# Seven quarter products in the second feed-forward of a two-layer decoder trunk

## The chip, the cores and the metric

The kernel runs on one core of one Trainium2 chip. The metric is the device time of one execution in microseconds, the median over several runs. TensorE (PE) multiplies matrices out of on-chip memory (SBUF) into accumulation banks (PSUM), VectorE (DVE) and ScalarE (ACT) work on elements, GpSimd (POOL) and SyncE (SP) issue transfers between main memory and SBUF here. Each engine takes its instructions in one fixed order and waits on semaphores for what the others produce.

## The reference

A sequence of 512 tokens of width 1024 goes through two layers. Each layer is a token mixer and then a feed-forward, each followed by a residual sum and a layer norm:

```python
x = layer_norm(DEEPNORM_ALPHA * x + mix, ln1_g[layer], ln1_b[layer])
ffn = sqrelu_mlp(x, ffn_w1[layer], ffn_b1[layer], ffn_w2[layer], ffn_b2[layer])
x = layer_norm(DEEPNORM_ALPHA * x + ffn, ln2_g[layer], ln2_b[layer])

def sqrelu_mlp(x, w1, b1, w2, b2):
    return jnp.square(jax.nn.relu(x @ w1 + b1)) @ w2 + b2
```

`w1` is 1024 x 4096 and `w2` 4096 x 1024, all in float32. The first layer's mixer is a state-space group beside stick-breaking attention, the second's a convolution module. The change concerns the second layer's feed-forward alone, above all its last product, squared hidden (512 x 4096) times `w2`.

## The kernel before

Every float32 product runs as three matmuls of a reduced 32-bit type. An operand is split into a high part (a cast on ScalarE, line 101 for weights, 215 for activations) and a low part, the rest (a subtraction on VectorE, lines 102 and 216); the product is high x high + low x high + high x low. One matmul takes a stationary 128 x 128 operand and streams 512 columns past it.

The inner dimension of 4096 is cut into 32 tiles of 128. In the second layer they go in blocks of 8, 8, 6, 4 and 6 (line 40). For each tile of a block `ffn1` (line 1033) computes the hidden tile, features by tokens, with 8 x 3 = 24 matmuls (`gemm`, line 219; named f in the profile), then Relu (ScalarE), square (VectorE) and the split. After that the block's part of the output product follows (line 1311, named g): tokens are the stationary operand, four token blocks of 128, and 512 output columns of `w2` stream by, once for each half of the columns. Each of the eight results (4 token blocks x 2 halves) is added by VectorE (line 1314) to one of eight tiles XT of 128 tokens x 512 columns, which hold the scaled residual. The last block (line 1327, named h) goes token block by token block, with the layer norm and the writing of its rows behind each.

Ahead of the first block stands the *lead*: while the layer norm of the second half of the tokens is computed, TensorE already does the first six hidden tiles (LEAD = 6; named fl), first for the one half of the tokens, then for the other. Then `residual` (line 1276) scales x and turns it into tokens by features with 32 transposes on TensorE (line 1284, named xt), copied to XT by ScalarE (line 1287).

Weights come through the class `Weights`: a list of units in the order of use, each 128 x 1024 elements. `next` hands out a unit and prepares those up to five ahead (`ahead`): load by SP (line 71, two buffers of 1 MB named raw), cast, subtraction, into a ring of eight slots. The order of the instructions on each engine is made by a scheduler when the program is built.

Of the kernel before, what the change touches and what calls it, by code (L numbers as in the profile page):

```python
# [39 lines left out]
FFN_BLOCKS = ((8, 8, 8, 8), (8, 8, 6, 4, 6))  # L40
# [15 lines left out]
class Weights:  # L56


    def __init__(self, tc, ahead):
        self.tc, self.nc, self.ahead = tc, tc.nc, ahead  # L60
        self.slots, self.units, self.raw, self.urgent, self.fence, self.hold = [], [], None, True, None, False
        self.done, self.got, self.chunk, self.ready, self.kept = 0, 0, {}, {}, {}

# [3 lines left out]
    def fetch(self, i):  # L67
        key, src, nk, ncol, off, width = self.units[i]
        if key not in self.chunk:
            self.chunk[key] = self.raw.tile([P, nk, width], F32, tag="raw", name=f"raw{i}", bufs=2)  # L70
            self.nc.sync.dma_start(self.chunk[key], src)
# [8 lines left out]
    def _prep(self, n):  # L80
        nc = self.nc
        while self.done < min(n, len(self.units)):
            key, src, nk, ncol, off, width = self.units[self.done]
            if key[0] == "split":
                pool, s = self.slots[self.done % len(self.slots)]
# [6 lines left out]
            self.fetch(self.done)  # L92
            raw = self.chunk[key][:, :, off : off + ncol]
            pool, s = self.slots[self.done % len(self.slots)]
# [12 lines left out]
            self.done += 1  # L107

# [57 lines left out]
def kernel(ctx: ExitStack, tc: tile.TileContext, a: dict, out: bass.AP):  # L166
# [63 lines left out]
    wpool = ctx.enter_context(tc.tile_pool(name="mw", bufs=1))  # L230
# [600 lines left out]
    wp2 = ctx.enter_context(tc.tile_pool(name="w2", bufs=1))  # L831
    hid = ctx.enter_context(tc.tile_pool(name="hid", bufs=1))
# [30 lines left out]
    for layer in range(2):  # L863
        if layer:
            units += [(("split", i), None, 8, 128, 0, 0) for i in range(24 + LEAD)]
        k0 = 0
        for nb in FFN_BLOCKS[layer]:
            for m in range(k0, k0 + nb, 4):
                units += units_of(f"f1{layer}", a["ffn_w1"][layer], 0, 8, range(max(m, LEAD * layer) * P, min(m + 4, k0 + nb) * P, 128), 256)
                if layer == 0 and m >= KEEP_FROM:  # L870
# [3 lines left out]
            for j in range(0, KT, 4) if layer == 0 else ():  # L874
# [6 lines left out]
            if layer == 0:  # L881
                pass
            else:
                for c in (0, 512):
                    for k in range(k0, k0 + nb, 2):
                        units += units_of("f21", a["ffn_w2"][1], k, 2, [c], 512)
# [383 lines left out]
    W.ahead = AHEAD[0]  # L1270
    xs, first = tail_norm_lead(cs_, "d", None, ("ln1_g", 8), ("ln1_b", 8), LEAD, "fl1", the_rest)


    XT = [None] * KT

# [13 lines left out]
    def ffn2_tok(ps, hs, b, ws, f):  # L1289
# [91 lines left out]
```

## Time and profile before

| | |
|---|---|
| median of 3 runs | 1185.39 us (1182.16 to 1188.67) |
| profiled execution, first to last instruction | 1181.7 us; the page gives no other time for it |
| TensorE matmuls | busy 1154.5 us, 98% |
| VectorE | busy 752.0 us, 64% |
| ScalarE | busy 507.9 us, 43% |
| mean granted TensorE clock | 0.995 |
| second layer's feed-forward | from the lead's last part at 839.92 us to the end |

Busy matmuls are pipelined, so a busy TensorE is not one at its peak; the spacing of its matmuls is read from the chain of waits. An operation's mean duration is longer than the step from one to the next in a queue. Shares over the whole span mix stages, so the stretches from 840 us on are the ones to look at.

### The profile page before, as it was taken

To read this page: it belongs to the slowest core of one execution; us is meant where nothing else is said; L and a number is where in the kernel's file an instruction comes from. 1 tells how busy PE (TensorE), PEld (TensorE's weight loads), DVE (VectorE), ACT (ScalarE), POOL (GpSimd) and SP (SyncE) were. 2 spreads that over 40 slices of the span, in tenths; PEclk is the share of its full clock that TensorE was granted. 3 is DMA by queue.
4 is the path that set the end of the run, shared out by engine and by line. 5 is a ranking of instruction groups with operands and counts; after the bars stand their busy time and mean duration, and the time that the engine had idled before them with its cause. 6 is when DMAs were issued, how large, how long until landed. Compare 5 with 4: busy or idle time off the path is not lost.

```text
span 1181.7 us, 17927 instructions
## 1 busy us (share of the span) xinstructions
PE 1154.5 (98%) x7252; PEld 966.1 (82%) x7252; DVE 752.0 (64%) x1332; ACT 507.9 (43%) x802; POOL 66.5 (6%) x125
## 2 busy tenths in 40 slices
PE   9989999999999999999999999899999999999997
PEld 7777767799888888888999776699988888888885
DVE  7999875498546546546565999886933433434446
ACT  6857769345434435434323122662741422413220
POOL 1022210000000000000021110001000000000000
PEclk9999999999999999999999999999999999999999
DMA  8511221332689678788464641215242232323211
GB/s 211 166 55 50 81 81 46 109 114 72 223 292 299 228 281 298 249 292 290 134 213 153 205 164 58 68 44 172 90 143 72 89 125 72 109 91 104 78 47 72
DMA packets 132547, 169.60 MB, mean 144 GB/s; under 512 B 13874, under 2 KB 105778, under 8 KB 132464
## 3 DMA queue, kind: packets, MB, share of 16 engines
q1 hardware_dynamic: 123664, 136.96, 36.0%
q0 software_dynamic: 8640, 31.46, 7.9%
q8 instruction: 57, 0.93, 0.3%
q14 instruction: 26, 0.21, 0.1%
q10 hardware_dynamic: 160, 0.03, 0.0%
HBM read 132.12 MB, written 35.65 MB: 142 GB/s over the span
## 4 chain that ended last, share of the span: by engine, by line
PE 83%; ACT 2%; DVE 1%; DMA 1%; issue 1%; POOL 0%; SPq 0%; DVEq 0%; ACTq 0%
PE f L225 24%; PE g L1311 12%; PE acf L225 11%; PE fl L225 5%; PE tlb L225 4%; PE tld L225 4%; PE pv L225 3%; PE h L1295 3%; PE pg L225 3%; PE cw L1126 3%; PE tla L225 2%; PE pl L225 2%; PE acmo L225 1%; PE gg L225 1%; PE gv L225 1%
## 5 line engine op out<-in xcount | busy, mean ns | idle before, releaser
L102 DVE TENSOR_TENSOR wlo<-raw,whi 128x1024 fp32r<-128x1024 f32 x176 | 213.3, 1223 | 196.1 <-ACT whi L101 193.0
L101 ACT CAST whi<-raw 128x1024 fp32r<-128x1024 f32 x176 | 182.3, 1050 | 319.6 <-PE g L1311 107.0
L1311 PE MATMUL g<-whi,hh 128*128 128x512 f32 x208 | 81.7, 393 | 0.0
L1311 PE MATMUL g<-whi,hl 128*128 128x512 f32 x208 | 81.6, 392 | 0.0
L1311 PE MATMUL g<-wlo,hh 128*128 128x512 f32 x208 | 81.6, 392 | 0.0
L225 PE MATMUL f<-xah,whi 128*128 128x512 f32 x208 | 81.0, 390 | 0.0
L225 PE MATMUL f<-xdh,whi 128*128 128x512 f32 x208 | 81.0, 389 | 0.0
L225 PE MATMUL f<-xdl,whi 128*128 128x512 f32 x208 | 80.9, 389 | 0.0
L225 PE MATMUL f<-xal,whi 128*128 128x512 f32 x208 | 80.9, 389 | 0.0
L225 PE MATMUL f<-xdh,wlo 128*128 128x512 f32 x208 | 80.9, 389 | 0.0
L225 PE MATMUL f<-xah,wlo 128*128 128x512 f32 x208 | 80.9, 389 | 0.0
L225 PE MATMUL acf<-hh,whi 128*128 128x512 f32 x192 | 75.6, 394 | 0.0
L225 PE MATMUL acf<-hl,whi 128*128 128x512 f32 x192 | 75.5, 393 | 0.0
L225 PE MATMUL acf<-hh,wlo 128*128 128x512 f32 x192 | 75.4, 393 | 0.0
L215 ACT CAST hh<-fr 128x512 fp32r<-128x512 f32 x64 | 39.7, 621 | 59.1 <-DVE fr L353 59.1
L216 DVE TENSOR_TENSOR hl<-fr,hh 128x512 fp32r<-128x512 f32 x64 | 44.1, 690 | 31.1 <-ACT hh L215 31.1
L353 DVE TENSOR_TENSOR fr<-fr 128x512 f32<-128x512 f32 x64 | 43.6, 684 | 16.7 <-ACT fr L154 16.7
L357 DVE SCALAR_TENSOR_TENSOR cy<-hp,wdw,cy 128x512 f32<-128x512 f32 (+1 forms) x75 | 49.3, 657 | 0.8 <-ACT cy L154 0.8
L88 POOL DMA_DIRECT2D whi<-kepth x30 | 16.0, 535 | 549.5 <-PE tlb L225 385.9
L1311 PEld LDWEIGHTS g<-whi,hh 128*128 128x128 f32 x208 | 39.1, 188 | 8.8
L1311 PEld LDWEIGHTS g<-wlo,hh 128*128 128x128 f32 x208 | 39.1, 188 | 8.8
L1311 PEld LDWEIGHTS g<-whi,hl 128*128 128x128 f32 x208 | 39.0, 188 | 8.8
(631 smaller groups left out, 2891.9 us busy)
## 6 DMA issues: line engine op xcount, KB each, us to landing
raw<-in_ffn_w_dram SPq DMA_DIRECT2D x48, 1024.0 KB, 5.5
raw<-in_ffn_w_dram SPq DMA_DIRECT2D x32, 512.0 KB, 3.8
kepth<-whi SPq DMA_DIRECT2D x30, 512.0 KB, 3.2
keptl<-wlo SPq DMA_DIRECT2D x30, 512.0 KB, 9.2
whi<-kepth POOLq DMA_DIRECT2D x30, 512.0 KB, 3.6
wlo<-keptl POOLq DMA_DIRECT2D x30, 512.0 KB, 4.6
raw<-in_conv_w_pw_dram SPq DMA_DIRECT2D x12, 1024.0 KB, 6.5
raw<-in_mix_w_in_dram SPq DMA_DIRECT2D x16, 512.0 KB, 4.2
```

The costliest lines, as they stand in the source:

```text
L88: nc.gpsimd.dma_start(x, d)
L101: i0 = nc.scalar.copy(hi, raw).ins
L102: i1 = nc.vector.tensor_sub(lo, raw, hi.bitcast(F32)).ins
L215: i0 = S.copy(hi, src).ins
L216: i1 = V.tensor_sub(lo, src, hi.bitcast(F32)).ins
L225: ins = PE.matmul(ps[:, c0:c1], u[:, k, ksl], v[:, c0:c1], start=start and k == 0 and i == 0, stop=stop and k == n - 1 and i == 2).ins
L353: V.tensor_tensor(o, x, y, op=op)
L357: V.scalar_tensor_tensor(o, x, s, y, op0=op0, op1=op1)
L1126: PE.matmul(cps[j, c0][g][C, :], Ds[j][t // 16][R, t % 16, :], hps[j][R, t + c0 : t + c1], start=t < 4, stop=t >= n - 4, tile_position=(R. ...
L1295: PE.matmul(ps, u, v, start=k == 0 and i == 0, stop=k == nk - 1 and i == 2)
L1311: PE.matmul(pss[b], u, v[:, kk, :], start=k + kk == 0 and i == 0, stop=k + kk == nb - 1 and i == 2)
```

## The change

For the first 24 of the 32 inner tiles the output product is formed after Strassen's identity. The blocks are now 6, 6, 6, 6 and 8. In a block of six the tiles are taken as three pairs (e = 0, 1). A pair's hidden tile is split by token half, the weights by the pair's tile and by column half, so that a 2 x 2 times 2 x 2 block product arises, formed from seven quarter products in place of eight. A quarter product of a block is 2 token blocks x 3 pairs x 3 = 18 matmuls.

- On the hidden side (`pair`) a tile q of 8 slots of 256 tokens holds the four quarters and four sums or differences; seven of them are split into high and low, three in one cast and one subtraction (768 elements), four in another (1024). The square moved from VectorE to ScalarE.
- On the weight side four quarters of 128 x 3 x 512 elements are loaded per block by SP (`load_quads`); `operand` forms four differences in place on VectorE, and each of the seven operands is split (1536 elements). The ring has four slots, `ahead` is 3.
- `seven` goes through the products in the order 1, 2, 5, 6, 3, 7, 4. Product 3 goes on adding into the bank of product 5, products 7 and 4 into that of product 6, and VectorE adds a bank to XT after each step, 12 sums per block. Product 1 is collected in R1 and added to all eight XT tiles in the last block of six.
- The pools of the weights are closed and three new ones opened at the turn to the second layer's feed-forward. Hidden weights there are loaded in single units of 512 KB.
- Block 0 has only the lead's six hidden tiles. The last block, of eight tiles, does the first column half for all token blocks, then the second by token block.

```diff
-FFN_BLOCKS = ((8, 8, 8, 8), (8, 8, 6, 4, 6))
+FFN_BLOCKS = ((8, 8, 8, 8), (6, 6, 6, 6, 8))
+ORDER7 = (1, 2, 5, 6, 3, 7, 4)
+NB = 6
+NSLOT = 4
...
+            if key[0] == "quad":
+                raw = self.operand(*key[1:])
+            else:
+                self.fetch(self.done)
+                raw = self.chunk[key][:, :, off : off + ncol]
...
+    def load_quads(self, blk, w2, k0, nb):
+        src = w2[k0 * P : (k0 + nb) * P].rearrange("(k e p) (f n) -> e f p k n", e=2, p=P, f=2)
+        q = self.quads[blk] = {}
+        for e, f in ((0, 0), (1, 0), (0, 1), (1, 1)):
+            q[e, f] = self.raw.tile([P, nb // 2, T], F32, tag=f"quad{e}{f}", name=f"quad{blk}{e}{f}", bufs=1)
+            self.nc.sync.dma_start(q[e, f], src[e, f])
+    def operand(self, blk, i):
+        q, sub = self.quads[blk], self.nc.vector.tensor_sub
+        b11, b12, b21, b22 = q[0, 0], q[0, 1], q[1, 0], q[1, 1]
+        if i == 5:
+            sub(b11, b12, b11)
+        elif i == 6:
+            sub(b11, b22, b11)
+        elif i == 7:
+            sub(b12, b22, b12)
+        elif i == 4:
+            sub(b21, b21, b11)
+        return {1: b11, 2: b21, 5: b11, 6: b11, 3: b22, 7: b12, 4: b21}[i]
...
+    def turn():
+        wst.close()
+        pools = [ctx.enter_context(tc.tile_pool(name=f"w3{x}", bufs=1, reuse_waits="tile")) for x in "abc"]
+        W.slots, W.base, W.raw, W.ahead = [], W.done, pools[1], NSLOT - 1
...
+    def pair(m, pss):
+        q = f1.tile([P, 8, H], F32, tag="q", name=f"q{m}", bufs=2)
+        hi, lo = (f1.tile([P, 7, H], F32R, tag=f"a{x}", name=f"a{x}{m}", bufs=NB // 2) for x in "hl")
+        for e in range(2):
+            r = rect(m + e, pss[e] if pss else hidden(m + e)).rearrange("p (h c) -> p h c", h=2)
+            act(q[:, 1:3] if e else q[:, 0:8:7], r, AF.Square)
+        split_part(hi[:, 0:3], lo[:, 0:3], q[:, 0:3])
+        tt(q[:, 3], q[:, 7], q[:, 2], ALU.add)
+        tt(q[:, 4], q[:, 3], q[:, 0], ALU.subtract)
+        tt(q[:, 5], q[:, 0], q[:, 7], ALU.subtract)
+        tt(q[:, 6], q[:, 1], q[:, 4], ALU.subtract)
+        split_part(hi[:, 3:7], lo[:, 3:7], q[:, 3:7])
+        return hi, lo
...
+    def seven(blk, As, first, final):
+        for i in ORDER7:
+            wh, wl = W.next()
+            chain = {3: 5, 7: 6, 4: 6}.get(i, i)
+            for t in range(2):
...
+                for p, (ah, al) in enumerate(As):
+                    uh, ul = ah[:, PLACE[i], c], al[:, PLACE[i], c]
+                    for n_, (u, v) in enumerate(((uh, wh), (ul, wh), (uh, wl))):
+                        PE.matmul(ps, u, v[:, p, :], start=chain == i and p == 0 and n_ == 0, stop=p == len(As) - 1 and n_ == 2,
+                                  skip_group_check=True)
...
+                    for x in (2 * t, 2 * t + 1, 2 * t + 4, 2 * t + 5) if final else ():
+                        tt(XT[x], XT[x], R1[t], ALU.add)
+                else:
+                    x = 2 * t + {2: 0, 5: 5, 6: 1, 3: 1, 7: 5, 4: 4}[i]
+                    tt(XT[x], XT[x], ps, ALU.add)
...
     k0 = 0
-    for bi, nb in enumerate(FFN_BLOCKS[1]):
-        hs = ffn1(1, bi, k0, nb, xs, stp, first if bi == 0 else ())
+    for bi, nb in enumerate(FFN_BLOCKS[1][:-1]):
+        if bi:
+            W.load_quads(k0, a["ffn_w2"][1], k0, nb)
+        As = [pair(m, first[m : m + 2] if bi == 0 else None) for m in range(k0, k0 + nb, 2)]
         if bi == 0:
             residual()
+        seven(k0, As, bi == 0, bi == len(FFN_BLOCKS[1]) - 2)
```

Up to the end of the lead every engine's order is the same in both kernels, but for two weight units that ScalarE and VectorE prepared there before and no longer do. Three places of the new order follow; line numbers are those of the changed kernel.

ScalarE, after the lead's last hidden tile (fl15, turned to r15). Names: q4 and ah4 are the third pair's tile and its high parts, xt the transposed X, whi152 and whi153 the high parts of the first two quarter weights. In the changed kernel:

```order
L185 ACTIVATE r15_8689<-fl15_8447,PV_86 128x512
L185 ACTIVATE q4_8683<-r15_8689 128x512
L1356 CAST ah4_8684<-q4_8683 128x768
L1337 COPY X0_61<-xt00_8716 128x512
L1337 COPY X1_62<-xt10_8717 128x512
L1337 COPY X2_63<-xt20_8718 128x512
L1356 CAST ah4_8684<-q4_8683 128x1024
L110 CAST whi152_8635<-quad000_8627 128x1536
L1337 COPY X3_64<-xt30_8719 128x512
L1337 COPY X4_65<-xt01_8740 128x512
L110 CAST whi153_8639<-quad010_8629 128x1536
```

Before, the same stretch was this, with TensorE at hidden tiles 6 and 7 (f16, f17) meanwhile:

```order
L154 ACTIVATE fr15_8661<-fl15_8447,PV_86 128x512
L101 CAST whi158_8727<-raw158_8725 128x1024
L215 CAST hh15_8664<-fr15_8661 128x512
L101 CAST whi159_8832<-raw159_8830 128x1024
L154 ACTIVATE fr16_8717<-f16_8668,PV_86 128x512
```

The copies of X have moved up, and the first weights of the product stand behind them.

VectorE in the first block of products (wlo152 to wlo156: low parts of the weights of products 1, 2, 5, 6 and 3; quad: the differences; X: sums into the output):

```order
L111 TENSOR_TENSOR wlo152_8636<-quad000_8627,whi152_8635 128x1536
L111 TENSOR_TENSOR wlo153_8640<-quad010_8629,whi153_8639 128x1536
L131 TENSOR_TENSOR quad000_8627<-quad001_8631,quad000_8627 128x1536
L135 TENSOR_TENSOR quad001_8631<-quad011_8633,quad001_8631 128x1536
L111 TENSOR_TENSOR wlo156_8797<-quad011_8633,whi156_8796 128x1536
L111 TENSOR_TENSOR wlo154_8766<-quad000_8627,whi154_8765 128x1536
L385 TENSOR_TENSOR X0_61<-X0_61,s020_8800 128x512
L133 TENSOR_TENSOR quad000_8627<-quad011_8633,quad000_8627 128x1536
L385 TENSOR_TENSOR X1_62<-X1_62,s021_8810 128x512
L111 TENSOR_TENSOR wlo157_8824<-quad001_8631,whi157_8823 128x1536
L111 TENSOR_TENSOR wlo155_8771<-quad000_8627,whi155_8770 128x1536
```

Of this only the sums into X were there before. The low parts for product 3 (wlo156) and product 7 (wlo157) stand ahead of those that products 5 and 6 need first.

TensorE in the last block of products (s186: bank of product 6, s185: of products 5 and 3, f124: hidden tile 24):

```order
L1390 MATMUL s1861_10147<-whi194_10045,al22_9970 128x512
L1390 MATMUL s1861_10147<-wlo194_10046,ah22_9969 128x512
L256 MATMUL f124_10239<-xdh0_7955,whi198_10161 128x512
L256 MATMUL f124_10239<-xdl0_7956,whi198_10161 128x512
L1390 MATMUL s1850_10110<-whi195_10079,ah18_9813 128x512
L1390 MATMUL s1850_10110<-whi195_10079,al18_9814 128x512
```

Two of the 24 matmuls of tile 24 stand between products 6 and 3; the other 22 follow after product 4. Before, hidden tiles and output products did not mix.

More of the change, by code (lines that the diff above doesn't have):

```diff
@@ L873 @@
                     n += 2
-            for j in range(0, KT, 4) if layer == 0 else ():
+            for j in range(0, KT, 4):
                 units += units_of("f20", a["ffn_w2"][0], k0, nb, range(j * P, (j + 4) * P, 128), 256)
@@ L880 @@
                     n += m
[L881 to L886, printed above, removed]
             k0 += nb
@@ L1287, in residual @@
                 S.copy(X[4 * f + b], pss[b])
-    def ffn2_tok(ps, hs, b, ws, f):
-        nk = len(hs)
-        for k in range(nk):
-            hh, hl = (t_[:, b * P : (b + 1) * P] for t_ in hs[k])
-            wh, wl = (t_[:, k % 2, :] for t_ in ws[k // 2])
-            for i, (u, v) in enumerate(((hh, wh), (hl, wh), (hh, wl))):
-                PE.matmul(ps, u, v, start=k == 0 and i == 0, stop=k == nk - 1 and i == 2)
+    hst.close()
+    f1 = ctx.enter_context(tc.tile_pool(name="f1", bufs=1, side="right", reuse_waits="tile"))
@@ new lines, with rect, hidden, split_part @@
+    R1 = [page(f"R1{t}", F32) for t in range(2)]
+    def rect(m, ps):
+        r = page(f"r1{m}", F32)
+        act(r, ps, AF.Relu, bias=pv("ffn_b1", 32 + m))
+        return r
+    def hidden(m):
+        ps = stp(f"f1{m}")
+        gemm(ps, W.next(), slice(0, P), xs, 0, T)
+        return ps
+    def split_part(hi, lo, src):
+        S.copy(hi, src)
+        V.tensor_sub(lo, src, hi.bitcast(F32))
+    def pair(m, pss):
[11 more added lines that the diff above has]
+        return hi, lo
@@ new lines @@
+    PLACE = {1: 0, 2: 1, 4: 2, 5: 3, 6: 4, 7: 5, 3: 6}
+    def seven(blk, As, first, final):
+        bank = {}
+        for i in ORDER7:
+            wh, wl = W.next()
+            chain = {3: 5, 7: 6, 4: 6}.get(i, i)
+            for t in range(2):
+                if chain == i:
+                    bank[i, t] = nps(f"s{blk}{i}{t}")
+                ps = bank[chain, t]
+                c = slice(t * P, (t + 1) * P)
+                for p, (ah, al) in enumerate(As):
[3 more added lines that the diff above has]
+                                  skip_group_check=True)
+            for t in range(2):
+                ps = bank[chain, t]
+                if i == 1:
+                    if first:
+                        S.copy(R1[t], ps)
+                    else:
+                        tt(R1[t], R1[t], ps, ALU.add)
+                    for x in (2 * t, 2 * t + 1, 2 * t + 4, 2 * t + 5) if final else ():
+                        tt(XT[x], XT[x], R1[t], ALU.add)
+                else:
+                    x = 2 * t + {2: 0, 5: 5, 6: 1, 3: 1, 7: 5, 4: 4}[i]
+                    tt(XT[x], XT[x], ps, ALU.add)
@@ L1316 @@
+    hs = []
+    for i in range(nb_last):
+        if i % 3 == 0:
+            hl_ = [f1.tile([P, 3, T], F32R, tag=f"a{x}", name=f"b{x}{i}", bufs=NB // 2) for x in "hl"]
+        r = rect(k0 + i, hidden(k0 + i))
+        act(r, r, AF.Square)
+        hs.append(tuple(x[:, i % 3, :] for x in hl_))
+        split_part(*hs[-1], r)
     gb = []
```

85 lines of the change are left out of this document (53 added, 32 removed).

## The prediction

> **What bounds the kernel now.** I read the page's busy times first, then busy time by stretch, then the chain of waits.
>
> ```profile
> span 1181.7 us, 17927 instructions
> ...
> PE 1154.5 (98%) x7252; PEld 966.1 (82%) x7252; DVE 752.0 (64%) x1332; ACT 507.9 (43%) x802; POOL 66.5 (6%) x125
> ```
>
> ```profile
> 850.00:900.00 50.00, 49.98 (x241) 41.47 (x240) 20.06 (x24) 18.71 (x26) 0.00 (x0) 1.00 0.40 127
> 900.00:950.00 50.00, 50.00 (x221) 41.20 (x220) 22.18 (x26) 17.29 (x22) 0.00 (x0) 1.00 0.27 84
> 1050.00:1100.00 50.00, 50.00 (x220) 40.94 (x219) 21.52 (x25) 14.28 (x17) 0.00 (x0) 1.00 0.31 96
> ```
>
> In these stretches of the second feed-forward (busy PE, PEld, DVE, ACT, POOL, then granted clock and DMA) TensorE has no hole at the full clock, VectorE is busy 40 to 44% of the time, ScalarE 29 to 37%. The chain that ended last, in order of time, is TensorE from the lead's end to the final layer norm:
>
> ```profile
> 839.92 11.28 PE fl L225 x94
> 851.20 10.91 PE f L225 x48
> 862.11 2.62 PE xt L1284 x24
> 864.73 0.02 issue
> 864.75 1.15 PE xt L1284 x8
> 865.90 44.28 PE g L1311 x192
> ...
> 1030.48 33.00 PE g L1311 x144
> ...
> 1140.21 33.26 PE h L1295 x144
> ```
>
> So here the time is the number of matmuls times their spacing: 10.91/48 = 0.227 us for a hidden tile's (f), 44.28/192 = 0.231 us for an output product's (g, h). Each matmul removed is 0.231 us, as long as the vector work stays under the matmuls.
>
> **What it removes.** Over 24 inner tiles the output product is 24 x 8 x 3 = 576 matmuls. Now each pair of tiles takes seven products of 2 x 3 matmuls: 12 x 42 = 504, of the same shape. The last eight tiles keep their 192. So 72 matmuls go: 72 x 0.231 = **16.6 us**. The hidden tiles' and the 32 transposes stay as they were.
>
> **What it adds, per block of six tiles.** The nearest rows, by group and in order of time:
>
> ```profile
> L102 DVE TENSOR_TENSOR wlo<-raw,whi 128x1024 fp32r<-128x1024 f32 x56 | 68.6, 1225 | 135.8 <-ACT whi L101 134.2 <-PE xt L1284 1.4 <-PE fl L225 0.2
> ...
> L353 DVE TENSOR_TENSOR X<-X,g 128x512 f32<-128x512 f32 x32 | 21.9, 686 | 11.6 <-PE g L1311 11.2
> ```
>
> ```profile
> L101 ACT CAST whi<-raw 128x1024 fp32r<-128x1024 f32 x56 | 58.9, 1052 | 162.8 <-PE g L1311 107.0 <-PE f L225 51.3 <-DMA raw<-in_ffn_w_dram 4.5
> L215 ACT CAST hh<-fr 128x512 fp32r<-128x512 f32 x32 | 19.9, 623 | 32.1 <-DVE fr L353 32.1
> ```
>
> ```profile
> 820.51 1.42 DVE L353 TENSOR_TENSOR sqd<-sqd,sqd 128x256 f32<-128x256 f32 x4
> 834.77 2.35 DVE L102 TENSOR_TENSOR wlo<-raw,whi 128x1024 fp32r<-128x1024 f32 x2
> 837.04 3.69 DVE L353 TENSOR_TENSOR X<-xdh,xdl 128x512 f32<-128x512 f32 x6
> ```
>
> Operations of 1536 elements (the quarter weights) are in no row. From 512 to 1024 elements VectorE's two-tensor operation grows by 1.225 - 0.686 = 0.54 us, ScalarE's cast by 0.43. Bounds: VectorE 1.225 (no growth) to 2.45 (two of 1024), ScalarE 1.05 to 2.10. I take the straight line, **1.76 and 1.48 us**, since 512 and 1024 lie on one with a small constant; 768 elements likewise 0.96 and 0.84. In a queue the next operation starts about 0.1 us before the end of the last (two of 1024 take 2.35, six of 512 take 3.69), so a wide one costs 1.66 there, one of 512 elements 0.60, one of 256 0.36.
>
> VectorE per block: hidden weights 6 x 1.225 = 7.4; three pairs of tiles at 4 x 0.36 + 0.96 + 1.225 = 3.6, so 10.9; quarter weights, seven low parts and four differences, 11 x 1.76 = 19.4; sums into the output 14 x 0.69 = 9.7. Together 47.4 us, beside 144 x 0.227 + 126 x 0.231 = 61.8 us of TensorE. On average it stays hidden, at 77%, but it is bunched. I went through the new order of each engine at the three places where bunches meet TensorE, on the profile's clock.
>
> ```profile
> 851.33 0.69 ACT L154 ACTIVATE fr<-fl,PV 128x512 f32<-128x512 f32 x1
> ...
> 866.07 2.57 ACT L1287 COPY X<-xt 128x512 f32<-128x512 f32 x5
> ```
>
> *Start of the first block.* The lead ends at 851.2. Before, two hidden tiles (10.91 us) covered the vector work that follows. Now block 0 has exactly the lead's six tiles, and only the transposes are left, 2.62 + 1.15 = 3.8 us, to 855.0. The first product waits for the high part of its weights, which stands on ScalarE behind the last lead tile's Relu (0.7), a square (0.65, between the copy's and the Relu's), a cast of 768 (0.75 in the queue), three copies of transposed X (0.51 each), a cast of 1024 (0.95); with its own 1.5 it is there at 857.3: **hole 2.3**. Four matmuls (0.9) later the low part (1.76) is not there: **0.8**. From 859.7, when ScalarE has the next cast done behind two more copies, five wide operations stand on VectorE before the third product's low part: 859.7 + 5 x 1.66 + 0.1 = 868.1; TensorE has 36 matmuls for it from 859.1, to 867.4: **0.8**. The fourth product's difference stands behind a sum, so its cast ends at 868.1 + 0.6 + 1.76 + 1.48 = 871.95, when TensorE, 14 matmuls on, has waited since 871.4: **0.5**. Its low part comes after sum, difference, sum and two low parts, 0.6 + 1.66 + 0.6 + 1.66 + 1.76 = 6.3 later, at 874.4, with 4 matmuls to 872.9: **1.5**. Then the block runs through. Sum 5.9 us.
>
> *From hidden tiles to products, three times.* TensorE has 26 matmuls of ready pairs before it needs the last pair's first low part. From the end of the last hidden tile but one that is 5.44 + 6.0 = 11.4 us. The other engines have in that time, one behind the other: Relu 0.7, a wide cast 1.5, four wide vector operations 6.7, two of 256 elements 0.7, one of 768 1.0, and some six handovers; 10.9 to 11.5 with these. No margin: I take **0.25 each, 0.8 us**.
>
> *In the last block of products.* Two matmuls of tile 24 stand between products 6 and 3; their weights' slot is that of product 6, which has just been read, so a cast of 1.05 lies bare: **1.05**. Product 3 adds onto the bank of product 5 and must wait for VectorE's sum from it, and in this block eight sums (8 x 0.60) stand ahead: from the end of product 1, R 0.6, 1.1, 4.8, 1.7, two sums 1.2, 1.7, 0.7 and handovers, 12.2 us, against TensorE's 42 x 0.231 + 1.05 + 0.46 = 11.2: **1.0**.
>
> A handover itself costs 0.05 to 0.15 us (ScalarE's gt ends at 84.10, VectorE's cl at 127.83):
>
> ```profile
> 83.52 0.58 ACT L524 COPY gt<-gp 128x512 f32<-128x512 f32 x1
> ...
> 84.15 1.65 PE L549 MATMUL vI<-U,gt 128*128 128x128 f32 x6 [2.05 <-ACT gt L524]
> ```
>
> ```profile
> 127.15 0.68 DVE L216 TENSOR_TENSOR cl<-av,ch 128x512 fp32r<-128x512 f32 x1
> ...
> 127.98 0.65 PE L723 MATMUL av<-w1C,vt 128*64 128x256 f32 x4 [1.45 <-DVE cl L216]
> ```
>
> For ten holes I add 0.5. Holes in all: 5.9 + 0.8 + 2.05 + 0.5 = **9.3 us**.
>
> Costed at nothing: *the loads.*
>
> ```profile
> raw<-in_ffn_w_dram SPq DMA_DIRECT2D x48, 1024.0 KB, 5.5
> raw<-in_ffn_w_dram SPq DMA_DIRECT2D x32, 512.0 KB, 3.8
> ```
>
> SP issues in order, and the weights of the third hidden tile of a block stand behind four quarter loads of 768 KB, the last of which waits for the previous block's last low part. That is done by the time product 4 starts; the tile is 18 + 48 matmuls away, 15 us, and needs one landing (5.5), a cast and a low part (2.3). If landing took twice as long it would still be covered. *The tail*: VectorE's work on a token block, from its last sum to the end of its last output row, is
>
> ```profile
> 1148.54 0.69 DVE L353 TENSOR_TENSOR X<-X,h 128x512 f32<-128x512 f32 x1 [2.74 <-PE h L1295]
> ...
> 1152.02 1.41 DVE L357 SCALAR_TENSOR_TENSOR X<-X,bmv,gb 128x512 f32<-128x512 f32 x2
> ```
>
> 4.9 us, now under 24 matmuls (5.5) instead of 36; uncovered it would be under 1 us.
>
> **Sum**: -16.6 + 9.3 = -7.3 us. The profiled span 1181.7 becomes 1174.4; the median of the runs shown, 1185.39, lies 3.7 above that span, so the time is **1178.1 us**. With holes between 7 and 11.5 us it is 1175.8 to 1180.3.
>
> **Rivals.** *B, the holes cool TensorE's clock.* Here the trace shows both:
>
> ```profile
> 82.00:84.00 2.00, 0.10 (x1) 0.00 (x0) 1.94 (x5) 1.00 (x3) 0.60 (x2) 1.00 0.00 0
> 84.00:86.00 2.00, 1.85 (x9) 1.85 (x9) 1.66 (x3) 0.27 (x2) 1.21 (x2) 0.53 0.03 8
> 86.00:88.00 2.00, 2.00 (x11) 1.91 (x9) 1.29 (x2) 0.00 (x0) 0.00 (x0) 0.62 0.10 25
> ...
> 742.00:744.00 2.00, 0.56 (x34) 0.48 (x34) 2.00 (x6) 0.00 (x0) 0.00 (x0) 1.00 0.00 0
> ```
>
> After the hole of 2.05 us up to 84.15 the granted clock is 0.53 and 0.62 for two slices of 2 us, which loses (0.47 + 0.38) x 2 = 1.7 us of matmuls; after a hole at 742 (0.56 busy of 2.00) it stays 1.00. The first hole, 2.3 and 0.8 us around 0.9 of work, is as long; but the later holes of that block (2.8 us) are set by VectorE and take such a loss up. What counts is the pair at the end, 2.05 us around 0.46 of work, and perhaps once more at the start: 2 x 1.7 = 3.4, so -3.9, **1181.5 us**. [...]
>
> *C, the wide vector operations are cheap* (1.225): the holes of VectorE vanish, those of ScalarE and of the slot stay, 2.3 + 0.3 + 0.4 + 1.05 = 4.0: -12.6, **1172.8 us**. Against it: both rows grow with the elements.
>
> *D, slower: VectorE's wide operations become the bound.* Eight stand in its queue ahead of the last pair at each of the three switches, nine in the first block's start, two ahead of the last block's sum: 24 + 9 + 2 = 35 on the path, with no margin left. Every 0.1 us by which one is dearer than 1.76 costs 3.5. From 1.97 on the gain is gone, from 2.14 the kernel is over 0.5% slower; at 2.2, within my bound of 2.45, +15.4 - 7.3 = +8.1, **1193.5 us**. For it: three of the strides are new (rows of three, in place). Against: the line through 512 and 1024. The same price holds for anything else that delays VectorE's queue there.
>
> That the matmuls don't fall away can't be: the new order has 504.
>
> **How the numbers follow.** Chances: forecast 0.52, B 0.22, C 0.10, D 0.16. A measurement of this kernel tells about 0.5%, 5.9 us: faster is below 1179.5. The forecast lies below it in seven cases of ten (0.37), C wholly (0.10), B seldom (0.04): faster 0.51. Same: the rest of the forecast 0.15, B 0.18, the near part of D 0.03, together 0.36; slower 0.13. The range of 8 in 10 runs from near C, 1174, into the first half of D, 1188; the forecast's own is 1175.8 to 1180.3.
>
> **What would show it.** Right: product matmuls in the Strassen blocks still 0.231 us apart and 504 of them; holes of TensorE before the first product (about 2.3, ScalarE's cast named) and some 3.5 us more within the next 20, named VectorE; two holes of about 1 us some 110 us before the end; none over 0.5 us elsewhere. Wrong: subtractions of 1536 elements away from 1.76 us (C, D); granted clock under 1 after 857 or in the last products (B); idle TensorE at hidden tiles with a DMA named (loads); VectorE idle while TensorE waits, since then the order was not what held it.

## The result, and the profile after

| | before | changed |
|---|---|---|
| median of 6 runs each | 1186.54 us (1182.01 to 1188.67) | 1176.17 us (1172.98 to 1178.04) |
| ratio, with its 95% interval | | 0.9915 (0.989 to 0.994) |
| profiled execution's span | 1181.7 us | 1171.2 us (this execution took 1172.98 us) |
| first matmul behind the lead | 851.0 us | 847.3 us |
| from there to the end of the span ("the stretch") | 330.7 us | 323.9 us |

The kernel is faster by 0.85%, and 1176.2 us stands beside the predicted 1178.1. The last two lines of the table are what the reasons have to be held against: of the 10.5 us between the two spans only 6.7 lie behind the lead, where the change is. The other 3.8 lie ahead of it, where both kernels have the same order of instructions; the experiments come back to them.

The head of the page of the changed kernel, as quoted for the kernel before:

```profile
span 1171.2 us, 17896 instructions
...
PE 1138.9 (97%) x7180; PEld 953.1 (81%) x7180; DVE 822.9 (70%) x1396; ACT 551.7 (47%) x838; POOL 67.0 (6%) x125
```

72 matmuls fewer, VectorE 71 us busier, ScalarE 44. The chain that ended last (start, length, what), behind the start of block 0:

```profile
872.00 17.31 PE s L1390 x68
889.31 32.64 PE f L256 x144
921.95 28.85 PE s L1390 x126
...
1064.03 12.54 PE s L1390 x54
1076.57 43.07 PE f L256 x190
1119.64 43.53 PE h L1436 x192
```

From hidden tiles (f) to products (s) and back TensorE runs through without a break: 889.31 + 32.64 is 921.95, where the products begin, and so it is in the two blocks that follow. A block's 126 product matmuls take 28.85 us, 0.2290 each. All of TensorE's waits behind the lead, grouped by what ended them (total us, times, longest):

```profile
PE s L1390 <- ACT whi L110: 2.5, 2, 2.2
PE s L1390 <- DVE wlo L111: 2.3, 3, 1.2
PE f L256 <- ACT whi L110: 1.0, 1, 1.0
PE s L1390 <- DVE X L385: 0.8, 1, 0.8
PE xt L1334 <- ACT X L1337: 0.2, 1, 0.2
```

and one by one, from TensorE's timeline (start, length, instruction, in brackets the idle time before it and what ended it):

```profile
853.51 0.50 PE L1390 MATMUL s<-whi,ah 128*128 128x512 f32 x1 [2.15 <-ACT whi L110]
...
855.30 0.80 PE L1390 MATMUL s<-wlo,ah 128*128 128x512 f32 x1 [0.57 <-DVE wlo L111]
...
865.79 0.50 PE L1390 MATMUL s<-wlo,ah 128*128 128x512 f32 x1 [0.53 <-DVE wlo L111]
...
869.58 0.50 PE L1390 MATMUL s<-whi,ah 128*128 128x512 f32 x1 [0.32 <-ACT whi L110]
...
872.00 0.62 PE L1390 MATMUL s<-wlo,ah 128*128 128x512 f32 x1 [1.23 <-DVE wlo L111]
```

```profile
1062.51 0.50 PE L256 MATMUL f<-xdh,whi 128*128 128x512 f32 x1 [0.95 <-ACT whi L110]
1064.03 0.50 PE L1390 MATMUL s<-whi,ah 128*128 128x512 f32 x1 [0.79 <-DVE X L385]
```

Five holes at the start of block 0 and two in the last block of products, in the places and with the engines that the prediction names; none at the three switches. TensorE's granted clock around these holes (stretch, its length, matmuls busy, clock, DMA):

```profile
851.75:855.16 3.41, 1.22 (x4) 1.00 0.00 0
855.16:858.57 3.41, 3.27 (x8) 0.50 0.00 0
868.81:872.23 3.42, 1.88 (x7) 1.00 0.88 255
872.23:875.64 3.41, 3.41 (x9) 0.50 0.59 211
```

The clock is halved from 855.16 to 858.57, which loses 3.41 x 0.5 = 1.7 us; it is halved a second time for as long from 872.23. After the two holes of the last block it stays 1.00. The wide operations of blocks 1 to 3, low parts on VectorE and casts on ScalarE, by group between 889 and 1060 us (times as in the page's fifth part: busy, mean ns):

```profile
L111 DVE TENSOR_TENSOR wlo<-quad,whi 128x1536 fp32r<-128x1536 f32 x19 | 33.3, 1754 | 2.8 <-ACT whi L110 2.6
L110 ACT CAST whi<-quad 128x1536 fp32r<-128x1536 f32 x21 | 30.7, 1478 | 13.6 <-PE f L256 8.0 <-PE s L1390 5.6
```

1.75 and 1.48 us, where the prediction took 1.76 and 1.48 from the straight line.

### The profile page after: what moved, and what is told of

Its sections match the earlier page's. It is cut to its first block, busy times and chain, and to the rows that moved or that the text cites. A ratio compares the mean times of both kernels' runs of the same rounds, so it can differ in the third digit from the quotient of the medians.

```text
span 1171.2 us, 17896 instructions
## 1 busy us (share of the span) xinstructions
PE 1138.9 (97%) x7180; PEld 953.1 (81%) x7180; DVE 822.9 (70%) x1396; ACT 551.7 (47%) x838; POOL 67.0 (6%) x125
## 4 chain that ended last, share of the span: by engine, by line
PE 82%; DVE 9%; ACT 4%; issue 2%; DMA 2%; POOL 0%; SPq 0%; DVEq 0%; ACTq 0%; POOLq 0%
PE f L256 24%; PE acf L256 11%; PE s L1390 8%; PE fl L256 5%; PE tlb L256 4%; PE tld L256 4%; PE h L1436 4%; PE pv L256 3%; PE pg L256 3%; PE cw L1165 3%; PE tla L256 2%; PE acmo L256 2%; PE pl L256 2%; DVE wlo L111 1%; PE gg L256 1%
## 5 line engine op out<-in xcount | busy, mean ns | idle before, releaser
L110 ACT CAST whi<-raw 128x1024 fp32r<-128x1024 f32 (+1 forms) x150 | 156.7, 1061 | 257.9 <-PE acf L256 61.0
L111 DVE TENSOR_TENSOR wlo<-raw,whi 128x1024 fp32r<-128x1024 f32 (+1 forms) x150 | 183.8, 1238 | 123.9 <-ACT whi L110 120.5
L1390 PE MATMUL s<-whi,ah 128*128 128x512 f32 x168 | 66.0, 400 | 3.3 <-ACT whi L110 2.5
L1390 PE MATMUL s<-wlo,ah 128*128 128x512 f32 x168 | 66.4, 402 | 2.3 <-DVE wlo L111 2.3
L1390 PE MATMUL s<-whi,al 128*128 128x512 f32 x168 | 66.0, 396 | 0.0
L111 DVE TENSOR_TENSOR wlo<-quad,whi 128x1536 fp32r<-128x1536 f32 x28 | 49.0, 1754 | 4.7 <-ACT whi L110 4.4
L110 ACT CAST whi<-quad 128x1536 fp32r<-128x1536 f32 x28 | 41.0, 1478 | 21.9 <-PE f L256 8.0
L256 PEld LDWEIGHTS f<-xdh,whi 128*128 128x128 f32 x208 | 39.0, 188 | 9.4 <-ACT whi L110 1.4
L256 PEld LDWEIGHTS f<-xah,whi 128*128 128x128 f32 x208 | 39.0, 188 | 8.2
L256 PEld LDWEIGHTS f<-xdh,wlo 128*128 128x128 f32 x208 | 39.0, 188 | 8.2
```

Of the source, the lines that this page charges most:

```text
L110: i0 = nc.scalar.copy(hi, raw).ins
L111: i1 = nc.vector.tensor_sub(lo, raw, hi.bitcast(F32)).ins
L256: ins = PE.matmul(ps[:, c0:c1], u[:, k, ksl], v[:, c0:c1], start=start and k == 0 and i == 0, stop=stop and k == n - 1 and i == 2).ins
L1390: PE.matmul(ps, u, v[:, p, :], start=chain == i and p == 0 and n_ == 0, stop=p == len(As) - 1 and n_ == 2, skip_group_check=True)
```

## The experiments

The questions: where do the 3.8 us ahead of the lead's end come from; does the clock's loss reach the end, or do later holes take it up (the prediction's case); is there really no margin at the switches, so that VectorE's queue is priced at 3.5 us per 0.1 us; and are the holes the two or three causes that they are put down to. For each kernel: median, ratio to the kernel before on the same chip, first matmul behind the lead, stretch from there to the end, and how often the clock was halved in block 0 of the profile.

| kernel | us (runs) | ratio to before (95%) | lead | stretch | halvings |
|---|---|---|---|---|---|
| before | 1186.54 (6) | | 851.0 | 330.7 | |
| before, once more (e9) | 1182.22 (1) | | 849.5 | 331.0 | |
| e1: pool of activations at the other end | 1181.38 (10) | 0.998 (0.997 to 0.999) | 848.9 | 329.3 | |
| e1 once more (e10) | 1180.65 (1) | | 849.6 | 329.3 | |
| changed | 1176.17 (6) | 0.9915 (0.989 to 0.994) | 847.3 | 323.9 | 2 |
| changed, once more (e8) | 1173.98 (4) | 0.992 (0.989 to 0.995) | 850.7 | 321.1 | 0 |
| e2: first hole filled | 1173.13 (4) | 0.991 (0.988 to 0.994) | 850.6 | 321.1 | 0 |
| e2 once more (e11) | 1177.40 (1) | | 854.6 | 321.1 | 0 |
| e3: squares on VectorE | 1177.01 (10) | 0.995 (0.993 to 0.997) | 854.9 | 325.6 | 2 |
| e4: last sums later | 1171.48 (4) | 0.991 (0.987 to 0.994) | 848.0 | 320.2 | 1 |
| e5: first casts earlier | 1170.57 (4) | 0.988 (0.985 to 0.991) | 855.9 | 315.3 | 0 |
| e6: spare work on VectorE | 1176.20 (4) | 0.994 (0.991 to 0.996) | 848.6 | 324.9 | 1, long |
| e7: e5 and e4 together | 1167.90 (4) | 0.986 (0.983 to 0.989) | 850.2 | 312.9 | 0 |

### e1, e9, e10: place in memory, or scatter

```diff
-    hid = ctx.enter_context(tc.tile_pool(name="hid", bufs=1))
+    hid = ctx.enter_context(tc.tile_pool(name="hid", bufs=1, side="right"))
```

> The kernel before, with one thing of the change alone: the pool of the activations (hid) lies at the other end of the on-chip memory. Every engine's order stays as it was. In the changed kernel the lead ended at 847.4 us in place of 851.2, with the same order of instructions up to there, and this kernel is to tell why. Theory 'place in memory': the 3.8 us come from where the tiles lie, so the lead ends at about 847.4 and the time is about 1182.7 (ratio 0.997). Rival 'scatter': executions of one kernel differ by that much ahead of the feed-forward; then the ratio is 1.000 within 0.002, and the lead's end lies anywhere between about 846 and 852. In both cases the stretch from the lead's end to the end of the span stays 330.5 us, with the output products' matmuls 0.2306 to 0.231 us apart; if the spacing falls to 0.227 to 0.229 as in the changed kernel, that part too is a matter of place.

> The kernel before, unchanged, one more profiled execution, beside the next one on the same chip. Theory 'place in memory sets the spacing': from the lead's end to the end of the span again 330.5 to 330.8, the last block's products (h) 33.26 us for 144 matmuls, 0.231 us apart, as in the first profile. Rival 'the spacing differs between executions': h at 32.65 (0.227) as with the activations' pool at the other end, the stretch 329.3. The lead's end lies anywhere from 847 to 856 in both.

> The kernel before with the activations' pool at the other end, once more. By 'place in memory' the stretch from the lead's end is again 329.3 and h 32.65 us; by the rival it lies where the kernel before lies, or anywhere between.

Both theories have a part. The chain of the kernel before, profiled once more (e9), and of the one with the moved pool (e10):

```profile
1139.01 33.26 PE h L1295 x144
```

```profile
1138.05 32.65 PE h L1295 x144
```

The products' matmuls come closer together where the activations lie elsewhere: h from 0.231 to 0.2267 us, and all five stretches of products from 176.95 to 175.70 us. The figures of e9 are those of the first profile of before, and those of e10 those of e1, to 0.03 us, so this is no scatter. The stretch is 1.4 us shorter (330.7 and 331.0 against 329.3 twice); the ratio of 0.998 fits that. So some 1.4 us can be had without Strassen's identity, by the place to which the change also moved the activations. The lead's end is scatter: it lay between 847.3 and 854.6 in the ten profiles of kernels whose order up to there is that of these two, for the kernel before at 851.0 and 849.5. The first profile of the changed kernel was at the early end of that, and its 3.8 us are no effect of the change. That also tells how a gain of this size has to be read: from the stretch, not from the span.

### e8, e2, e11: the clock in block 0

e8 is the changed kernel without an edit. e2 and e11 are one kernel, with matmuls in the first hole:

```diff
+    def warm(tr):
+        w = stp("warm")
+        for i in range(9):
+            fill.append(PE.matmul(w, xs[0][0][:, :P], xs[i % KT][0], start=i == 0, stop=i == 8))
...
-                    PE.transpose(pss[b][:, i * P : (i + 1) * P], X[4 * f + i][:, b * P : (b + 1) * P], ident)
+                    tr = PE.transpose(pss[b][:, i * P : (i + 1) * P], X[4 * f + i][:, b * P : (b + 1) * P], ident)
+            if f:
+                warm(tr)
```

> The changed kernel with nine more matmuls of 512 columns (2.04 us of work whose result nobody reads) right behind the transposes, in the hole of 2.15 us before the first product. Nothing else moves. Theory 'the clock counts': the granted clock of 0.50 after 855.2 comes from the hole; with TensorE busy there it stays 1.00 up to the third product, product 1 ends 1.6 us earlier, and since ScalarE's copy of R1 and the casts behind it wait for product 1, all that follows is 1.6 us earlier (3.2 if the second halving at 872 goes too): the stretch from the lead's end to the end of the span 320.5 to 322.3 in place of 323.8. Rival 'the later holes take it up' (as the prediction had it): product 1 ends earlier, but the wait at 872 grows by as much, and the stretch stays 323.6 to 324.0. If the clock is halved all the same, an idle TensorE isn't what halves it.

> The changed kernel as it is, beside the others on the same chip. If the lead's end scatters between executions whatever the kernel, it lies elsewhere than at 847.3 (847 to 855 was seen with the same order of instructions), while the stretch from there to the end of the span repeats: 323.9 with two halvings of the clock in block 0, 322.3 with one. If instead the place in memory sets it, the lead ends again at about 847.3.

> The changed kernel with the nine matmuls in the hole before the first product, once more. Without them the granted clock was halved in block 0 in four of five profiles of kernels that have this hole (twice, twice, once, once and not at all). If the hole is what halves it, there is no halving before the third product here either, and the stretch from the lead's end is 321 (or 322.5 with the second halving after the wait of 1.2 us); if it is chance, a halving shows up in most executions of this kernel too.

With the hole filled the clock stayed 1.00, twice, and the stretch was 321.1, twice, as the theory that the clock counts has it. But e8 shows that this alone proves little. The same holes, in one more execution of the changed kernel (timeline, then the clock in stretches of 3.41 us):

```profile
856.97 0.50 PE L1390 MATMUL s<-whi,ah 128*128 128x512 f32 x1 [2.15 <-ACT whi L110]
858.76 0.50 PE L1390 MATMUL s<-wlo,ah 128*128 128x512 f32 x1 [0.58 <-DVE wlo L111]
```

```profile
852.66:856.07 3.41, 1.98 (x16) 1.00 0.00 0
856.07:859.49 3.42, 1.94 (x7) 1.00 0.00 0
859.49:862.90 3.41, 3.41 (x17) 1.00 0.00 0
```

No halving, and again 321.1. So the holes don't always cool the clock: in five profiles with this hole (the changed kernel, e3, e4, e6, e8) it was halved twice, twice, once, once and not at all, in four with the hole filled or nearly gone (e2, e11, e5, e7) never.

The traces tell more when they are cut into steps of 3.413 us, the length of a halving. Between 30 and 1160 us the changed kernel's first profile shows the clock halved from 83.75, 855.16 and 872.23 us, for 3.413 us each; the second and third start lie 226 and 231 times 3.413 us behind the first. In the kernel before it is halved from 84.12 and 159.21 us, as long each, 22 times 3.413 us apart. With the steps counted from the first halving, those ahead of these five halvings had 1.33, 1.22 and 1.88 us of busy matmuls in the changed kernel and 1.38 and 1.34 before. Five other steps had less than 2 us and were followed by the full clock: 1.93, 1.83 and 1.82 in the changed kernel, 1.96 and 1.78 before. So from 1.78 to 1.88 it went both ways. In e8 the end of a step at 856.07 cuts the hole of 2.15 us in two, the steps on both sides have 1.98 and 1.94 us, and the full clock followed both. In e2 the step from 855.17 was busy for 2.83 us; by the hole's place in e8 some 1.7 us of that are the added matmuls, so without them it would be 1.1 (an estimate), less than ahead of any of the five halvings. For e11 the same estimate gives 1.9 us in both steps that the hole would touch, so e11 decides nothing. The reading that fits these figures is that the hole is the cause where most of it falls into one step, as it did in the changed kernel's first execution and not in e8; more than that these few steps don't show.

What a halving costs is shown: the changed kernel's two profiles differ by it alone, 323.94 - 321.08 = 2.9 us for two halvings that lose 3.4 us of matmuls.

Why the loss reaches the end can be read from the chain of the changed kernel's first profile:

```profile
855.30 4.99 PE s L1390 x14
...
860.32 0.02 ACT R L1396
...
860.80 1.49 ACT whi L110
...
872.00 8.02 PE s L1390 x27
```

ScalarE's copy of product 1's result (R) stands in its queue ahead of the third cast, and waits for the end of product 1; the cast, the low part, the sum, the difference and two low parts follow. So in this execution the chain passes through TensorE, and VectorE's queue waits for the third cast:

```profile
862.31 3.43 DVE L111 TENSOR_TENSOR wlo<-quad,whi 128x1536 fp32r<-128x1536 f32 x2 [1.20 <-ACT whi L110]
```

In e8, at the full clock, it does not. There VectorE's five wide operations behind the second cast follow one another, the two low parts right behind the two differences (the third cast is done at about 864.2, just ahead of its use):

```profile
859.29 1.76 DVE L111 TENSOR_TENSOR wlo<-quad,whi 128x1536 fp32r<-128x1536 f32 x1 [0.59 <-ACT whi L110]
...
864.48 3.42 DVE L111 TENSOR_TENSOR wlo<-quad,whi 128x1536 fp32r<-128x1536 f32 x2
```

The copies of R thus form a second chain, a little shorter than VectorE's queue, which takes over when product 1 is late. From the first matmul behind the lead to the end of the hole before 872.00 it was 24.7 us with the halved clock and 23.4 without (e8: 850.72 to 874.16), so 1.3 of the 1.7 us that product 1 lost came through.

### e5: the first two casts earlier

```diff
-        act(r, ps, AF.Relu, bias=pv("ffn_b1", 32 + m))
+        i = act(r, ps, AF.Relu, bias=pv("ffn_b1", 32 + m))
+        if m in {2: 0, 3: 1, 4: 1, 5: 1}:
+            tc.add_manual_dep(i, W.casts[W.turn[0] + {2: 0, 3: 1, 4: 1, 5: 1}[m]].name, NOSYNC, reason="behind a quarter's cast")
```

(`casts` holds the cast of each unit; the added dependence only fixes the order in ScalarE's queue.)

> The changed kernel with the casts of the first block's first two quarter weights moved ahead on ScalarE (before the Relu of the lead's third and fourth tile, in place of behind the copies of X); VectorE's low parts of them move along, everything behind block 0 stays. Theory 'the start hangs on ScalarE's order': in the changed kernel the holes of 2.15, 0.57, 0.53, 0.32 and 1.23 us in block 0 form one chain from the first cast (852.0) over product 1's end, the R1 copy and the third cast to the low part at 871.95. With the first cast earlier only holes at the transposes of together about 1 us remain, and the granted clock stays 1.00: 4.8 - 1.0 + 3.3 (two halvings of 1.65 each) = 7 us less, the stretch from the lead's end to the end of the span 316 to 318 in place of 323.9. Rival 'VectorE's queue holds the start' (the prediction's working): the five wide operations ahead of the third product's low part stay where they are, so the later holes grow by what the first loses; only the clock is won, and the stretch is 320 to 322.

TensorE's waits behind the lead:

```profile
PE f L256 <- ACT whi L110: 1.0, 1, 1.0
PE s L1391 <- DVE X L385: 0.8, 1, 0.8
PE s L1391 <- ACT X L1337: 0.6, 1, 0.6
```

The five holes and the short one at the transposes are one hole of 0.56 us; the stretch is 315.3, below the expected 316 to 318. The rival falls, since the wide operations did not stay where they were: two low parts and a difference now start at 851.26, 853.88 and 855.55, ahead of the lead's end at 855.9, and the scheduler rearranged what follows (six matmuls of the next block's first hidden tile stand ahead of product 4). That does not refute the prediction's working, after which the rival is named: the working starts VectorE's queue at the second cast, and e8 bears that out. What e5 shows is that the start depends on when the first casts are done, and that they and three of VectorE's wide operations fit into the lead. They do not lengthen it: from the first matmul of the first layer's lead to the last of the second's (both named fl) it is 589.7 us in e5 and 589.3 in e7, and 587.7 to 590.0 in the other eleven profiles.

Against the changed kernel without a halving (321.1) e5 gains 5.8 us, though the idle times that went add up to 0.17 + 2.15 + 0.58 + 0.75 + 0.32 + 1.23 - 0.56 = 4.6 there. The holes cost more than their named idle time. Two more rows of the changed kernel's timeline, between the matmuls at 853.51 and 855.30 shown above, tell how:

```profile
853.85 0.40 PE L1390 MATMUL s<-whi,al 128*128 128x512 f32 x1
...
854.33 0.40 PE L1390 MATMUL s<-whi,al 128*128 128x512 f32 x1
```

Behind the hole of 2.15 us the next matmul starts 0.34 us later in place of 0.23 (853.51 to 853.85), 0.11 more; and from the last start ahead of the hole of 0.57 to the first behind it are 0.97 us (854.33 to 855.30), 0.17 more than idle time and spacing. Together some 0.28 us, taken as an estimate for every hole: five holes fewer are 1.4 us, and 4.6 + 1.4 = 6.0 stands against the measured 5.8. The medians, 1173.98 and 1170.57 us, show only 3.4, with intervals that overlap; so the 5.8 rests on single profiles, of e8 and e5, and on e7's below.

### e4 and e7: the last sums, and both parts

```diff
-                    for x in (2 * t, 2 * t + 1, 2 * t + 4, 2 * t + 5) if final else ():
-                        tt(XT[x], XT[x], R1[t], ALU.add)
                 else:
                     x = 2 * t + {2: 0, 5: 5, 6: 1, 3: 1, 7: 5, 4: 4}[i]
                     tt(XT[x], XT[x], ps, ALU.add)
+                    if final and i == 4:
+                        gather(t)        # the four sums of R1[t]
```

> The changed kernel with the eight last sums of R1 into the output tiles (VectorE) moved from behind product 1 to behind product 4 of the last block of six; the first two matmuls of tile 24 thereby no longer stand between products 6 and 3. Theory 'the two holes are these two causes': both holes at 1062.5 (0.95, a weight's cast) and 1064.0 (0.79, the sum from product 5's bank) go, -1.7 us, the stretch from the lead's end to the end of the span 322.1. Rival 'moved, not removed': the eight sums (4.8 us of VectorE) come before the first low parts of the last eight tiles, and holes of the same size open there or at the first column half's products; the stretch stays 323.5 to 324.

> The changed kernel with both: the first two casts earlier and the eight last sums behind product 4. If the two parts are independent, the stretch from the lead's end to the end of the span is that of the first alone less 1.74 us (the holes of 0.95 and 0.79 in the last block): 314.5 to 316.5, against 323.9 in the changed kernel and 330.7 before; the ratio to the kernel before about 0.985. Rival: the block that starts without holes reaches a later wait sooner, and part of it opens again elsewhere (at the hidden tiles of the second block, named ScalarE): 317 to 319.

In e4 the waits named DVE X and the cast before f are gone; the last block of products and the hidden tiles behind it:

```profile
1044.17 28.86 PE s L1394 x126
1073.03 43.52 PE f L256 x192
```

It takes 28.86 us like the other blocks. In the changed kernel (e8) it begins at 1045.55 and the hidden tiles at 1077.15, 31.60 us with two hidden matmuls among them: 31.60 - 0.45 - 28.86 = 2.3 us for two holes of 0.95 and 0.76, that is 1.7 and twice 0.28. The two causes are the right ones, and nothing opened elsewhere: the stretch of 320.2 is 3.7 less than in the changed kernel's first profile, 2.3 for the holes and the rest for a second halving that this execution didn't have. e7 has both parts, and TensorE's only wait behind the lead is

```profile
PE s L1395 <- ACT X L1337: 0.6, 1, 0.6
```

Its stretch is 312.9, which is 315.3 - 2.3. At 1167.9 us (ratio 0.986, 0.983 to 0.989, where the changed kernel beside it has 0.992) it is the fastest of all; it beats the kernel before by 1.4%, and the changed kernel by 6 us, just as much as the two intervals tell apart.

### e3 and e6: what more work on VectorE costs

```diff
-            act(q[:, 1:3] if e else q[:, 0:8:7], r, AF.Square)
+            sq = q[:, 1:3] if e else q[:, 0:8:7]
+            tt(sq, r, r, ALU.mult)
```

> The changed kernel with one part undone: the 24 squares of the hidden tiles of the first four blocks are VectorE's again (0.60 us each in its queue), not ScalarE's. Theory 'no margin at the switches': in the changed kernel the last pair's first low part is ready at 927.77 and read at about 927.85, and VectorE worked for it without a gap from 919.34 on; one square more in that stretch puts a hole of 0.5 to 1.2 us at each of the three switches, and one of 0.5 to 0.7 more at the wait for the sum of product 5 in the last block: +2 to +4 us, the stretch from the lead's end 326 to 328. Rival 'queue with room': VectorE is busy 70% there and takes up the squares in its gaps of 0.7 to 1.1 us ahead of 919.34; holes at the switches under 0.3 us each, the stretch 323.8 to 324.8.

```diff
                 i1 = nc.vector.tensor_sub(lo, raw, hi.bitcast(F32)).ins
+                if key[0] == "quad":
+                    extra = nc.vector.tensor_sub(self.spare, raw[:, 0, : T // 2], hi.bitcast(F32)[:, 1, : T // 2]).ins
+                    self.tc.add_manual_dep(extra, i1.name, NOSYNC, reason="right behind it")
```

> The changed kernel with 28 more VectorE operations of 128x256 (0.36 us each in the queue, a result nobody reads), one behind the low part of each quarter weight. By the order four of them stand ahead of the last pair's first low part at each of the three switches, three ahead of the last low part that block 0 waits for, one or none ahead of the sum from product 5's bank in the last block. Theory 'no margin' (the price of the prediction's rival of dear wide operations: what is added to VectorE's queue is added to the time): 3 x 1.4 + 1.1 + 0.4, about +5 to +6 us, the stretch from the lead's end 329 to 330. Rival 'the queue has gaps ahead of its last stretch': VectorE waits 1.1, 1.1 and 0.7 us for ScalarE's casts in the 14 us ahead of a switch and works without a gap only for the last 8.4 us, where one spare operation stands: under 0.3 us per switch, +1.1 at the start: the stretch 325 to 326.5.

e3, TensorE's waits from 900 us on:

```profile
PE s L1391 <- DVE X L385: 1.4, 1, 1.4
PE f L256 <- ACT whi L110: 1.0, 1, 1.0
PE s L1391 <- ACT ah L1356: 0.7, 3, 0.3
```

The squares moved back open a hole of about 0.24 us at each switch and 0.6 more at the wait for the sum of product 5's bank: 1.3 us, with 0.28 for each new hole 2.2, and 325.6 - 323.9 = 1.7 (both with two halvings). That lies between the two theories: there was some margin, but the move of the squares was worth about 2 us. e6 has no hole at the switches at all; its longest in the last block are

```profile
1063.83 0.50 PE L259 MATMUL f<-xdh,whi 128*128 128x512 f32 x1 [0.95 <-ACT whi L110]
...
1066.29 0.50 PE L1394 MATMUL s<-whi,ah 128*128 128x512 f32 x1 [1.72 <-DVE X L388]
```

the second 0.9 more than before; at the start the holes of 0.53, 0.32 and 1.23 are 0.48, 0.64 and 1.24. The stretch is 324.9 with a halving that lasted two steps (3.4 us lost), so the 28 operations cost about 1 us, not 5 to 6. The margin at a switch is nevertheless small. In the changed kernel VectorE ahead of a switch, up to the last pair's first low part (al, 768), and the matmuls just ahead of its use:

```profile
905.61 1.23 DVE L1357 TENSOR_TENSOR al<-q,ah 128x1024 fp32r<-128x1024 f32 x1 [1.11 <-ACT ah L1356]
...
917.39 1.23 DVE L1357 TENSOR_TENSOR al<-q,ah 128x1024 fp32r<-128x1024 f32 x1 [1.12 <-ACT ah L1356]
919.34 1.76 DVE L111 TENSOR_TENSOR wlo<-quad,whi 128x1536 fp32r<-128x1536 f32 x1 [0.72 <-ACT whi L110]
...
925.15 1.75 DVE L111 TENSOR_TENSOR wlo<-quad,whi 128x1536 fp32r<-128x1536 f32 x1
926.82 0.95 DVE L1357 TENSOR_TENSOR al<-q,ah 128x768 fp32r<-128x768 f32 x1
```

```profile
927.67 0.65 PE L1390 MATMUL s<-whi,al 128*128 128x512 f32 x2
```

It is ready at 927.77, and TensorE, 26 matmuls of 0.227 behind 921.95, wants it at about 927.85. But VectorE has gaps of 1.1, 1.1 and 0.7 us up to 919.34, where it waits for ScalarE's casts; what is added before that is taken up there. And the order reacts: in e6 the added operation that belongs to the last quarter weight ahead of this switch stands behind the pair's low part (929.38 against 928.18), so it delays nothing. An operation that takes longer on the chip than the scheduler believes was not tried, and that is the case of which the rival of dear wide operations speaks.

## Why the prediction was right, and where it wasn't

The forecast of -7.3 us met -6.7 in the two first profiles, and its time lies 1.9 us above the measured median. That it lies so near is partly luck: the same kernel gave -9.6 in the execution without a halving (e8), and errors of both signs cancel. By its own steps:

- **What it removes: -16.6 forecast, -18.0 measured.** The products took 176.95 us before (g and h); now the four blocks, at the 28.86 us that they take without holes, and h with 43.53 make 158.97. The count was right; the spacing was taken as a constant of the operation, and it is none. It fell from 0.231 to 0.2290 and 0.2267, and e1, in the kernel before, gets 1.25 us of that from the place of the activations alone.
- **Wide operations: right.** 1.75 and 1.48 us, so rivals C and D have no ground.
- **Start of block 0: holes and reasons right at the full clock.** Forecast 2.3, 0.8, 0.8, 0.5 and 1.5 (the third and fourth are 0.7 and 0.6 by its own numbers, with the same sum of 5.9), measured 2.15, 0.58, 0.75, 0.32 and 1.23 in e8. From the lead's end the second cast was forecast at 859.7 - 851.2 = 8.5 us and done at 8.5, in e8 and in the first profile alike; the five wide operations behind it were put at 8.4 us and took 8.6 in e8. What the working lacks is the copies of product 1's result ahead of the third cast: with the clock halved they wait for TensorE, and the same five operations take 9.9 us (855.83 to 865.74). In that execution the holes were 2.15, 0.57, 0.53, 0.32 and 1.23, with 0.17 at the transposes 4.97 us.
- **The switches: 0.8 forecast, 0 measured.** The path was estimated at 10.9 to 11.5 us against 11.4, and it was met with 0.08 us to spare.
- **The last block: right.** 1.05 and 1.0 forecast, 0.95 and 0.79 measured, by the two causes named (e4).
- **Handovers: 0.5 forecast for ten holes, some 0.28 each by the estimate from two holes (e5)**, 2.2 us for eight. All holes together: 9.3 forecast, 6.7 measured + 2.2 = 8.9. The errors at the switches and at the handovers offset each other.
- **Rival B, the clock: where and when were wrong.** It was counted at the pair of holes at the end and left out at the start. In seven profiles with that last pair it was never halved there. The least busy step there had 2.33 us of matmuls in the changed kernel's first profile. In e6, with 0.95 and 1.72 us idle, it had 1.69, less than the 1.88 ahead of the halving at 872.23, and why the full clock followed it stays open. At the start it was halved in four of five, and the step that the later holes "are set by VectorE and take such a loss up" failed: they took up 0.4 of the first halving's 1.7 us, as the chain over the R copy shows. The forecast's sum lacked 0 to 2.9 us, by the execution.
- **Loads and tail at nothing: right.** No wait of TensorE names a DMA, and h ends 8.0 us before the span's end, against 8.2 before.

Sum in the terms measured: -18.0 + 8.9 + 2.9 = -6.2, and -0.2 at the tail, -6.4 against the measured -6.7. Without the halvings it is -9.3 against 321.1 - 330.7 = -9.6. The forecast lay between the two, with one term too small on the gain's side and one left out on the other; which execution was profiled first decided how near it came.

The 10.4 us between the medians lie in an interval of 7 to 13, which holds both -6.7 and -9.6; nothing ahead of the lead's end is needed to explain them.

## What to carry to other kernels

Where a kernel is bound by TensorE, fewer matmuls are worth their spacing only as far as the operands are ready (18.0 us of matmuls went here, and some 8.9 us of holes came), so go through each engine's queue at the places where one kind of work gives way to another. Prepare the first operands in the stretch before, where the engines have room: moving two casts was worth 5.8 us by the stretch, beside the 6.7 to 9.6 of the whole change. Look there too for an instruction that waits for TensorE itself (a copy out of a bank) with casts queued behind it, since such a chain hands a loss on (1.3 of 1.7 us here). Compare stretches that start at a common mark rather than spans, when what lies ahead scatters (by 7.3 us here, 847.3 to 854.6). And profile the same kernel twice before a halved clock is priced: with the same holes it was halved twice in one execution here and not at all in another, and 2.9 us hung on that.

## What the runs showed of the hardware that was not expected

- The spacing of the same matmul, 512 columns at the full clock, differed with the place of the activations: 0.231 us for h in the kernel before, 0.2267 with the pool of the activations at the other end, twice each.
- Between 30 and 1160 us the granted clock was halved three times in the changed kernel's first profile and twice in the kernel before, for 3.413 us each, the later ones 226, 231 and 22 times 3.413 us behind their profile's first. The steps of that length ahead of the five had 1.22 to 1.88 us of busy matmuls; every step with 1.93 us or more in these two profiles was followed by the full clock. In one more execution of the changed kernel (e8) the same holes, with 1.98 and 1.94 us in the steps around the first, halved nothing; in e6 the clock stayed halved for 6.8 us.
- The holes of TensorE cost about 0.28 us each beside the idle time that the profile names, an estimate from 0.11 us behind one of 2.15 and 0.17 us around one of 0.57. By it the five holes that e5 lacks make 6.0 us, where 5.8 was measured.
- With the same order of instructions the lead ended between 847.3 and 854.6 us in ten profiles. Most of that arises ahead of the first layer's lead, which began between 259.2 and 264.9 us in them.
